# Where the first loads are issued, and how the decay rows are formed, in a two-layer hybrid transformer kernel

## The chip, the cores and the metric

The kernel runs on one core of one Trainium2 chip. The metric is the device time of one execution in microseconds (us); the number given for a kernel is the median of its runs. One further execution was taken with the hardware profiler, and all rows below come from that one.

## The reference, cut to what matters

A sequence of 256 rows of width 2048 passes an even and an odd layer. Each layer normalizes its rows, multiplies by one wide weight matrix, runs three kinds of token mixing on slices of the product and multiplies by an output matrix:

```python
def even_layer(x, mem, ...):
    h = rms_norm(x, norm_g) @ w_in
    gq, gk, gv, gb, ga, gg, dq, dk, dv, dg, mq, mg = split_cols(h, EV_SPLITS)
    y = concat([gdn_branch(gq, gk, gv, gb, ga, gg, conv_w, a_log, dt_bias, gdn_gain),
                diff_attention(dq, dk, dv, dg, rel_table, dq_gain, dk_gain, lam, subln, lambda_init),
                memory_attention(mq, mg, mem, mem_norm, mem_w_kv, mem_qn, mem_kn)])
    return x + y @ w_out
# in gdn_branch, per head and chunk:  g = cumsum(g)
diff = g[..., :, None] - g[..., None, :]
decay = where(lower_incl, exp(where(lower_incl, diff, 0.0)), 0.0)
m = where(strict, einsum('bhncd,bhnsd->bhncs', k_beta, k) * decay, 0.0)
t_inv = triangular_solve(eye + m, eye)
a_intra = where(lower_incl, einsum('bhncd,bhnsd->bhncs', q, k) * decay, 0.0)
```

The odd layer has window attention and latent attention with rotary positions (cosines and sines of `positions`) in place of the first two, and memory attention again. `rel_bias` is the table behind the additive attention bias, `mem` the 256 memory rows. All is float32.

## The kernel before

**Products.** Every float32 product is made of three TensorE passes: each operand is split into a rounded high part and the remainder. `gemm` (L206 on) walks a weight matrix in blocks of 512 KB. A block is loaded by SyncE's queue (`load_w`, L194; four buffers `w`), cast to its high part `wh` on ScalarE (L201) and its low part `wl` formed on VectorE (L202; three buffers each), and then feeds 12 matmuls of 128x512: passes L218 (wh with xH), L219 (wl) and L220 (wh with xL). One 512-column product has eight such blocks. `gemm_T` does the same with the roles swapped (L233 to L235, 128x256).

**Order.** The program builds instructions in the order of the text, and a scheduler with its own timeline model then puts each engine's list into a fixed order; each engine, and each engine's DMA queue, takes its list strictly in that order. `tc.issue_after(x)` holds a scheduled instruction behind x. So an edit moves work on all engines, and an instruction that waits holds all that stands behind it on its engine.

**Start.** The transposed activations `xt` and the first weight blocks come through SyncE's queue; ScalarE and VectorE split `xt` into xH and xL (L154, L155). Behind the last split, ScalarE's queue issues the constants `cst` (128x672), a row of gains broadcast to 128 partitions (`bcp`, source `row`, 128x424), `hot`, `wrow`, `rel_bias` (`rbt`), `posi`, and the natural rows `xN` of x, twice 128x2048, for `natural_rms` (L180 to L187: one buffer `xnat`, sum of squares on ScalarE L186, then `inv_sqrt`: VectorE L144 and a power on GpSimd L145). Its result is `rs0`, the row scale. The first three products are the diff attention's q, k and v halves; `normed_T` (L261 on) squares the accumulators with `rs0` as scale (L269), reduces, takes a power on GpSimd, scales and transposes by TensorE. The hot table times `rel_bias` (one matmul, L456) is written to DRAM (L461) and read back as `bias` (L501, 1536 KB). The rotary tables `sn`, `cs` are two Sin on ScalarE (L488, L491), with a table load ahead of them. `mem_split` (L580 on) loads the transposed memory in eight pieces `mt` (two buffers, ScalarE's queue, L585) and splits them; `natural_rms` runs again over `memN`. L646 is the Exp of `ea`.

**Decay.** In the stage of the gated delta net, `keys_decay` runs for two groups of four heads. Per group, for both halves t of the rows and both directions d, it forms E = exp(g_c - g_r + mask): TensorE transposes a column of `gcum` broadcast to 128 columns (L757, tile `pb`), VectorE subtracts and adds the mask (L759, 128x128 each) and ScalarE takes the Exp (L761, 128x512). `pg` (L752) is k times k, and `MnT` (L763) their product. `MnT` of both groups goes through DRAM to a solver of 31 steps on VectorE (L787 on), whose inverses come back into `Tm` and `Rm` (L816, SyncE's queue; `Rm` is zeroed on GpSimd first, L804) for TensorE at L859 and later.

Of the kernel before, what the change touches and what calls it, by code (L numbers as in the profile page):

```python
# [87 lines left out]
def kernel(ctx: ExitStack, tc: tile.TileContext, a: dict, out: bass.AP):  # L88
# [332 lines left out]
    with tc.tile_pool(name="xn", bufs=8) as xn:
# [42 lines left out]
        lm = xn.tile([P, 2, 64], F32, name="lm", bufs=1)
        lv_ = bcp[:, B_LAM:B_LAM + 256].rearrange("p (a b c) -> p a b c", a=2, b=2)
        V.tensor_tensor(lm, lv_[:, :, 0], lv_[:, :, 1], op=ALU.mult)
        ls = spool.tile([P, 2], F32, tag="ls", name="ls")
        V.tensor_reduce(ls, lm, axis=AX.X, op=ALU.add)
        A.activation(ls, ls, AF.Exp)
        V.tensor_tensor(lamn, ls[:, 1:2], ls[:, 0:1], op=ALU.subtract)  # L470
        V.tensor_scalar(lamn, lamn, LAM0, None, op0=ALU.subtract)

        posf = xn.tile([P, 2], F32, name="posf", bufs=1)
        V.tensor_copy(posf, posi)
        ang, kk, red, sn, cs = [xn.tile([P, 2, 32], F32, name=n, bufs=1) for n in ("ang", "kk", "red", "sn", "cs")]
        V.tensor_tensor(ang, bcm(cst[:, C_IF:C_IF + 32], 2), bc3(posf, 32), op=ALU.mult)
        MAGIC = 1.5 * 2.0 ** 23
        V.tensor_scalar(kk, ang, 1.0 / (2 * math.pi), MAGIC, op0=ALU.mult, op1=ALU.add)
# [8 lines left out]
        V.tensor_scalar(red, red, pi_, -pi_, op0=ALU.min, op1=ALU.max)
        A.activation(sn, red, AF.Sin)  # L488
        V.scalar_tensor_tensor(red, red, -1.0, red, op0=ALU.mult, op1=ALU.max)
        V.tensor_scalar(red, red, -1.0, math.pi / 2, op0=ALU.mult, op1=ALU.add)  # L490
        A.activation(cs, red, AF.Sin)  # L491
        for i, (b0, sc_) in enumerate(((B_MQR, 192 ** -0.5), (B_MKR, 1.0))):
            g1, g2 = bcp[:, b0:b0 + 32], bcp[:, b0 + 32:b0 + 64]
            for j, (first, second) in enumerate(((cs, sn), (sn, cs))):
                V.scalar_tensor_tensor(tabs[:, :, 2 * i + j, 0:32], first, sc_, bcm(g1, 2), op0=ALU.mult, op1=ALU.mult)
                V.scalar_tensor_tensor(tabs[:, :, 2 * i + j, 32:64], second, sc_, bcm(g2, 2), op0=ALU.mult, op1=ALU.mult)
# [705 lines left out]
```

## Time and profile before

| | |
|---|---|
| runs | 1205.7, 1206.37, 1207.79 us (median 1206.37) |
| the profiled execution | 1208.67 us, of which the span of its instructions is 1206.9 us |
| granted TensorE clock, mean | 0.996 |
| busy, share of the span | PE 99%, PEld 88%, DVE 70%, ACT 53%, POOL 9% |
| chain that ended last, by engine | PE 89%, DVE 4%, DMA 3%, ACT 2% |

PE is TensorE's matmuls, PEld its weight loads, DVE VectorE, ACT ScalarE, POOL GpSimd, SP SyncE; a small q behind an engine's name is its queue of DMA issues. A matmul's span is modelled and overlaps the next one's, so a stretch with PE at 100% can still hold more or fewer matmuls than another: the number of instructions in a stretch of equal work tells more than the share.

### The profile page before, as it was taken

How to read it: one execution, taken by the hardware profiler on the slowest of the kernel's cores; microseconds unless marked ns; L12 is line 12 of the kernel's file. 1: busy time of each engine (PE TensorE's matmuls, PEld its weight loads, DVE VectorE, ACT ScalarE, POOL GpSimd, SP SyncE). 2: the span in 40 equal slices, each digit the busy share in tenths (PEclk: the TensorE clock that was granted, in tenths of full speed). 3: DMA queues.
4: the chain of work that ended last, by engine and by line, in shares of the span. 5: the costliest groups of instructions: out<-in, count | busy, mean ns of one | idle time of the engine just before them, and what ended most of it. 6: DMA issues, size and time to landing. Idle time of an engine off the chain costs nothing.

```text
span 1206.9 us, 19842 instructions
## 1 busy us (share of the span) xinstructions
PE 1190.3 (99%) x7608; PEld 1063.2 (88%) x7608; DVE 839.8 (70%) x1450; ACT 640.0 (53%) x1117; POOL 109.8 (9%) x116
## 2 busy tenths in 40 slices
PE   9899999999999999999999999999999999999998
PEld 7678888788999999889988889999889899998887
DVE  5675876666889899857755555667766678876553
ACT  6664666455555454444654446566555555554432
POOL 0110112000101010002000001323310000000000
PEclk9899999999999999999999999999999999999999
DMA  9976675555655666653536656666556565555663
GB/s 333 350 225 230 215 236 162 175 165 167 174 152 137 168 176 192 194 142 82 187 105 209 206 167 185 179 184 194 160 158 203 164 208 158 159 157 166 201 210 121
DMA packets 183183, 221.95 MB, mean 184 GB/s; under 512 B 20536, under 2 KB 119608, under 8 KB 182576
## 3 DMA queue, kind: packets, MB, share of 16 engines
q1 hardware_dynamic: 172640, 201.09, 56.0%
q10 hardware_dynamic: 9552, 16.48, 3.9%
q0 software_dynamic: 896, 3.11, 0.8%
q8 instruction: 59, 0.97, 0.3%
q14 instruction: 36, 0.29, 0.1%
HBM read 214.36 MB, written 6.29 MB: 183 GB/s over the span
## 4 chain that ended last, share of the span: by engine, by line
PE 89%; DVE 4%; DMA 3%; ACT 2%; issue 1%; POOL 1%; SPq 0%; DVEq 0%; ACTq 0%; POOLq 0%
PE acc L219 14%; PE acc L220 13%; PE acc L218 13%; PE acc L254 6%; PE acc L256 6%; PE acc L255 6%; PE acc L366 4%; PE acc L367 4%; PE acc L365 4%; PE acc L235 3%; PE acc L233 3%; PE acc L234 3%; PE ps L165 3%; PE ps L892 1%; DVE wl L202 1%
## 5 line engine op out<-in xcount | busy, mean ns | idle before, releaser
L202 DVE TENSOR_TENSOR wl<-w,wh 128x1024 fp32r<-128x1024 f32 (+3 forms) x392 | 456.8, 1167 | 240.5 <-ACT wh L201 237.9
L201 ACT CAST wh<-w 128x1024 fp32r<-128x1024 f32 (+3 forms) x392 | 392.1, 1001 | 401.4 <-PE acc L220 141.3
L219 PE MATMUL acc<-wl,xH 128*128 128x512 f32 (+3 forms) x704 | 259.5, 370 | 3.0 <-DVE wl L202 3.0
L220 PE MATMUL acc<-wh,xL 128*128 128x512 f32 (+3 forms) x704 | 256.0, 365 | 0.0
L218 PE MATMUL acc<-wh,xH 128*128 128x512 f32 (+3 forms) x704 | 238.5, 366 | 2.7 <-ACT wh L201 2.7
L219 PEld LDWEIGHTS acc<-wl,xH 128*128 128x128 f32 x704 | 133.1, 189 | 24.2 <-DVE wl L202 5.4
L218 PEld LDWEIGHTS acc<-wh,xH 128*128 128x128 f32 x704 | 130.5, 189 | 21.1 <-ACT wh L201 4.2
L220 PEld LDWEIGHTS acc<-wh,xL 128*128 128x128 f32 x704 | 133.1, 189 | 17.1
L255 PE MATMUL acc<-wl,y 128*128 128x512 f32 x320 | 124.9, 391 | 0.0
L256 PE MATMUL acc<-wh,y 128*128 128x512 f32 x320 | 124.4, 390 | 0.0
L254 PE MATMUL acc<-wh,y 128*128 128x512 f32 x320 | 115.3, 392 | 1.3 <-ACT y L154 1.3
L235 PE MATMUL acc<-xH,wl 128*128 128x256 f32 x384 | 109.4, 286 | 1.1 <-DVE wl L202 1.1
L365 PE MATMUL acc<-xH,wh 128*128 128x256 f32 x384 | 110.1, 287 | 0.0
L366 PE MATMUL acc<-xL,wh 128*128 128x256 f32 x384 | 109.9, 286 | 0.0
L367 PE MATMUL acc<-xH,wl 128*128 128x256 f32 x384 | 109.6, 286 | 0.0
L233 PE MATMUL acc<-xH,wh 128*128 128x256 f32 x384 | 109.3, 285 | 0.0
L234 PE MATMUL acc<-xL,wh 128*128 128x256 f32 x384 | 109.1, 284 | 0.0
L145 POOL TENSOR_TENSOR r<-isq,kept 128x4 f32<-128x4 f32 (+2 forms) x27 | 49.7, 1841 | 400.4 <-DVE isq L144 384.1
L235 PEld LDWEIGHTS acc<-xH,wl 128*128 128x128 f32 x384 | 73.4, 191 | 1.7 <-DVE wl L202 1.7
L366 PEld LDWEIGHTS acc<-xL,wh 128*128 128x128 f32 x384 | 74.2, 193 | 0.3
L365 PEld LDWEIGHTS acc<-xH,wh 128*128 128x128 f32 x384 | 74.3, 194 | 0.2
L367 PEld LDWEIGHTS acc<-xH,wl 128*128 128x128 f32 x384 | 74.1, 193 | 0.0
(364 smaller groups left out, 1760.9 us busy)
## 6 DMA issues: line engine op xcount, KB each, us to landing
w<-in_ev_w_in_dram SPq DMA_DIRECT2D x136, 512.0 KB, 4.1
w<-in_od_w_in_dram SPq DMA_DIRECT2D x72, 512.0 KB, 3.9
w<-in_ev_w_out_dram SPq DMA_DIRECT2D x40, 512.0 KB, 3.7
w<-in_od_w_out_dram SPq DMA_DIRECT2D x40, 512.0 KB, 4.1
w<-in_od_w_in_dram SPq DMA_DIRECT2D x32, 384.0 KB, 3.4
w<-in_od_mem_w_kv_dram SPq DMA_DIRECT2D x16, 512.0 KB, 3.6
w<-in_ev_mem_w_kv_dram SPq DMA_DIRECT2D x16, 512.0 KB, 3.7
w<-in_od_w_in_dram SPq DMA_DIRECT2D x16, 288.0 KB, 2.9
```

The source lines that it names most:

```text
L201: A.copy(wh[:, :kn * n], w[:, :kn * n])
L202: V.tensor_tensor(wl[:, :kn * n], w[:, :kn * n], wh[:, :kn * n].bitcast(F32), op=ALU.subtract)
L218: T.matmul(o, lhsT=h, rhs=wh[:, k], start=first, stop=False)
L219: T.matmul(o, lhsT=h, rhs=wl[:, k], start=False, stop=False)
L220: T.matmul(o, lhsT=l, rhs=wh[:, k], start=False, stop=last)
L235: T.matmul(o, lhsT=wl[:, k], rhs=H[:, kk], start=False, stop=kk == NK - 1)
L254: T.matmul(acc[t], lhsT=h, rhs=wh[:, k], start=first, stop=False)
L255: T.matmul(acc[t], lhsT=h, rhs=wl[:, k], start=False, stop=False)
L256: T.matmul(acc[t], lhsT=l, rhs=wh[:, k], start=False, stop=last)
L365: T.matmul(acc[i], lhsT=wh[:, k, cs], rhs=H[:, kk], start=kk == 0, stop=False)
L366: T.matmul(acc[i], lhsT=wh[:, k, cs], rhs=L[:, kk], start=False, stop=False)
L367: T.matmul(acc[i], lhsT=wl[:, k, cs], rhs=H[:, kk], start=False, stop=kk == NK - 1)
```

## The change

- `cst`, `row` and `xN` stay on ScalarE's queue, `xN` first, with two buffers for `xnat` so that both halves are issued back to back. `hot`, `wrow`, `rbt` and `posi` go to GpSimd's queue and are no longer held behind the last split.
- The memory pieces `mt` go to GpSimd's queue with eight buffers, held behind the power that forms `rs0` (`first_pow`). Their splits are held behind the norming of the keys (`normed[2]`, `normed[3]`: the third and fourth split that `normed_T` makes). The bias table's store is held behind `first_pow`, its load and `memN` behind `normed[2]`, the rotary tables and lambda behind `normed[3]`.
- E is formed otherwise: `gcum` is transposed once and stored to DRAM (`gc_d`); eight DMAs with a zero partition step load its rows broadcast to 128 partitions (128x512 each, ScalarE's queue); VectorE adds the mask (128x512), and ScalarE takes the Exp with -gcum as its bias (128x128 each).
- The memset of `Tm` is held behind that of the solver's identity.

```diff
+    def natural_rms(rs, src, pool, bufs, eng):
         ss = spool.tile([P, 2], F32, tag="ssx", name="ssx")
+        nat = []
         for t in range(2):
-            n_ = pool.tile([P, D], F32, tag="xnat", name="xnat", bufs=1)
-            A.dma_start(n_, src[t * P:(t + 1) * P, :])
+            nat.append(pool.tile([P, D], F32, tag="xnat", name="xnat", bufs=bufs))
+            eng.dma_start(nat[t], src[t * P:(t + 1) * P, :])
+        for t, n_ in enumerate(nat):
             A.activation(n_, n_, AF.Square, accum_out=ss[:, t:t + 1])
-        inv_sqrt(rs, ss, 1.0 / D, EPS)
+        return inv_sqrt(rs, ss, 1.0 / D, EPS)
...
-            split(src, gain, dst(0, t), dst(1, t))
+            normed.append(split(src, gain, dst(0, t), dst(1, t)))
...
         with tc.issue_after(last.ins):
+            first_pow = natural_rms(rs0, a["xN"], xn, 2, A)
             A.dma_start(cst, a["cst"])
             A.dma_start(bcp, a["row"].to_broadcast([P, B_END]))
-            A.dma_start(hot, a["hot"][0:32])
-            A.dma_start(wrow, a["hot"][32:40])
-            A.dma_start(rbt, a["rel_bias"])
-            A.dma_start(posi, a["positions"].rearrange("o (t p) -> p (o t)", p=P))
-            natural_rms(rs0, a["xN"], xn)
+        for dst, src in ((hot, a["hot"][0:32]), (wrow, a["hot"][32:40]), (rbt, a["rel_bias"]),
+                         (posi, a["positions"].rearrange("o (t p) -> p (o t)", p=P))):
+            G.dma_start(dst, src)
...
-        for i, row in enumerate((brow, wrow)):
-            G.dma_start(bias_d[i], row)
+        with tc.issue_after(first_pow.ins):
+            for i, row in enumerate((brow, wrow)):
+                G.dma_start(bias_d[i], row)
...
-                mt = dp.tile([P, 2, S], F32, tag="mn", name="mt")
-                with tc.issue_after(last.ins):
-                    A.dma_start(mt, mTsrc[:, 2 * g:2 * g + 2])
+                mt = dp.tile([P, 2, S], F32, tag="mn", name="mt", bufs=8)
+                with tc.issue_after(first_pow.ins):
+                    G.dma_start(mt, mTsrc[:, 2 * g:2 * g + 2])
                 for k in range(2):
                     kk = 2 * g + k
-                    split(mt[:, k], par[:, gr + kk:gr + kk + 1], mH[:, kk, :], mL[:, kk, :])
+                    with tc.issue_after(normed[2 + g // 4 if lay == 0 else 0].ins):
+                        split(mt[:, k], par[:, gr + kk:gr + kk + 1], mH[:, kk, :], mL[:, kk, :])
             if lay == 0:
-                with tc.issue_after(last.ins):
-                    natural_rms(rsm, a["memN"], dp)
+                with tc.issue_after(normed[2].ins):
+                    natural_rms(rsm, a["memN"], dp, 1, A)
...
+            ngcum = sm("ngcum")
+            V.tensor_scalar(ngcum, gcum, -1.0, None, op0=ALU.mult)
+            pt = ps_tile()
+            T.transpose(pt[:32, :P], gcum, ident)
+            gr = dp.tile([32, P], F32, name="gr", bufs=1)
+            V.tensor_copy(gr, pt[:32, :P])
+            G.dma_start(gc_d, gr)
...
+        E = gp.tile([P, 2, 2, 4, P], F32, tag="E", name="E", bufs=2)
+        for t in range(2):
+            for d in range(2):
+                r_ = gc_d[t * 16 + d * 8 + h0:t * 16 + d * 8 + h0 + 4]
+                with tc.issue_after(weighed[-1].ins):
+                    A.dma_start(E[:, d, t].rearrange("p h c -> p (h c)"), bass.AP(r_.tensor, r_.offset, [[0, P], [1, 4 * P]]))
...
             for d in range(2):
-                pb = ps_tile()
+                V.tensor_tensor(E[:, d, t], E[:, d, t], bcm(amask(d), 4), op=ALU.add)
                 for h in range(4):
-                    T.transpose(pb[:, h * P:(h + 1) * P], cols(gcum, t, d)[:, h:h + 1].to_broadcast([P, P]), ident)
-                for h in range(4):
-                    V.scalar_tensor_tensor(E[:, d, t, h], pb[:, h * P:(h + 1) * P], cols(gcum, t, d)[:, h:h + 1],
-                                           amask(d), op0=ALU.subtract, op1=ALU.add)
-                A.activation(E[:, d, t], E[:, d, t], AF.Exp)
+                    A.activation(E[:, d, t, h], E[:, d, t, h], AF.Exp, bias=cols(ngcum, t, d)[:, h:h + 1])
...
-        G.memset(Tm, 0.0)
+        with tc.issue_after(eye.ins):
+            G.memset(Tm, 0.0)
```

The scheduler then puts the lists into a new order. The rows below are the engines' fixed lists: line, operation, what it writes and reads, size. First ScalarE at the start, before, from the Exp of `ea` that waits for its constants (L646) to the cast of the weight block after the rotary Sin:

```order
L646 ACTIVATE kept<-kept 128x16
L585 DMA mt<-in_memT_dram 128x2x256
L201 CAST wh<-w 128x1024
L445 DMA wrow<-in_hot_dram 8x512
L469 ACTIVATE ls<-ls 128x2
L186 ACTIVATE xnat,ssx<-xnat 128x2048
L201 CAST wh<-w 128x1024
L185 DMA xnat<-in_xN_dram 128x2048
L186 ACTIVATE xnat,ssx<-xnat 128x2048
L488 ACT_TABLE_LOAD
L488 ACTIVATE sn<-red 128x64
L201 CAST wh<-w 128x1024
```

And ScalarE at the same place with the change, from the loads of `cst` and `row` (both `xN` stand just ahead of them) to the first splits of q. L188 is the sum of squares of `xN`, L273 the square that reads `rs0`; the cast ahead of the second L188 is that of the keys' first block:

```order
L448 DMA kept<-in_cst_dram 128x672
L449 DMA kept<-in_row_dram 128x424
L203 CAST wh<-w 128x1024
L188 ACTIVATE xnat,ssx<-xnat 128x2048
L203 CAST wh<-w 128x1024
L188 ACTIVATE xnat,ssx<-xnat 128x2048
L273 ACTIVATE sq<-acc,kept 128x512 x2
L203 CAST wh<-w 128x1024 x8
L154 ACTIVATE qT<-acc,kept 128x4x128 x2
```

The Sin and its table load, the memory's sums and the Exp of `ea` have left this place; the two squares that read `rs0` now stand ahead of eight casts, the first of them that of the keys' second block. In the list before, those squares stood five casts further on.

VectorE with the change, between the low parts of the weight blocks: `ang` reads `cst` and `posi`, `lm` reads `row`, and `isq` is the step of `rs0`:

```order
L204 TENSOR_TENSOR wl<-w,wh 128x1024 x3
L658 TENSOR_TENSOR ang<-kept,posf 128x64
L660 TENSOR_SCALAR kk<-ang 128x64
L661 TENSOR_SCALAR kk<-kk 128x64
L647 TENSOR_TENSOR lm<-kept 128x128
L665 SCALAR_TENSOR_TENSOR red<-kk,ang 128x64
L144 TENSOR_SCALAR isq<-ssx 128x2
```

So `rs0` stands behind the landings of `cst` and `row` too, and not of `xN` alone.

ScalarE with the change in the stage of the decay; L759 are the broadcasting loads of E, L780 the Exp, L203 the casts of weight blocks:

```order
L759 DMA E<-gc_d 128x512 x7
L736 ACTIVATE sqs<-ps 128x512
L739 COPY kN<-ps 128x512
L780 ACTIVATE E<-E,kept 128x128 x3
L736 ACTIVATE sqs<-ps 128x512
L739 COPY kN<-ps 128x512
L780 ACTIVATE E<-E,kept 128x128
L721 ACTIVATE kT<-cc 128x256
L203 CAST wh<-w 128x1024
L780 ACTIVATE E<-E,kept 128x128 x4
```

Seven loads are issued at once. On VectorE seven of the eight mask additions stand ahead of the low part of the block cast here, and on ScalarE 28 of the 32 Exp stand between this cast and the next.

## Rows read from the trace of the kernel before

**Rows 1.** The page: busy times; bytes moved, in 40 slices of 30.2 us.
```profile
PE 1190.3 (99%) x7608; PEld 1063.2 (88%) x7608; DVE 839.8 (70%) x1450; ACT 640.0 (53%) x1117; POOL 109.8 (9%) x116
...
GB/s 333 350 225 230 215 236 162 175 165 167 174 152 137 168 176 192 194 142 82 187 105 209 206 167 185 179 184 194 160 158 203 164 208 158 159 157 166 201 210 121
```

**Rows 2.** Waits of PE, whole run: total us, times, longest us.
```profile
PE acc L219 <- DVE wl L202: 3.0, 5, 1.0
PE acc L218 <- ACT wh L201: 2.7, 3, 1.9
PE ps L859 <- DMA Rm<-r_d: 2.3, 1, 2.3
```

**Rows 3.** Windows: us, busy by engine PE, PEld, DVE, ACT, POOL, then PEclk, DMA share, GB/s.
```profile
10.00:20.00 10.00, 10.00 (x45) 8.02 (x44) 9.71 (x16) 8.86 (x16) 0.00 (x0) 1.00 1.07 375
20.00:30.00 10.00, 10.00 (x45) 7.89 (x43) 3.98 (x7) 3.46 (x6) 0.00 (x0) 1.00 1.03 348
30.00:40.00 10.00, 7.18 (x28) 4.44 (x26) 6.88 (x22) 8.62 (x14) 1.28 (x2) 0.96 1.03 392
40.00:50.00 10.00, 9.96 (x31) 8.03 (x32) 7.12 (x15) 9.04 (x12) 0.72 (x1) 0.69 1.03 376
350.00:400.00 50.00, 50.00 (x428) 50.00 (x427) 48.07 (x130) 28.70 (x47) 4.58 (x2) 1.00 0.56 148
520.00:530.00 10.00, 8.15 (x191) 7.84 (x192) 4.83 (x7) 2.65 (x6) 0.00 (x0) 0.83 0.52 147
```

**Rows 4.** Timeline of PE: start, us, engine, line, tiles, count, [idle before <- releaser].
```profile
33.57 0.62 PE L218 MATMUL acc<-wh,xH 128*128 128x512 f32 x2
...
38.35 0.73 PE L218 MATMUL acc<-wh,xH 128*128 128x512 f32 x2 [1.90 <-ACT wh L201]
...
40.04 0.80 PE L219 MATMUL acc<-wl,xH 128*128 128x512 f32 x1 [0.96 <-DVE wl L202]
```

**Rows 5.** Timeline of ACT, 27 to 38 us.
```profile
27.88 0.22 ACT L646 ACTIVATE kept<-kept 128x16 f32<-128x16 f32 x1 [5.37 <-DMA xnat<-in_xN_dram]
...
37.27 1.03 ACT L201 CAST wh<-w 128x1024 fp32r<-128x1024 f32 x1
```

**Rows 6.** Waits of SyncE's queue, 0 to 70 us.
```profile
SPq L194 <- DMA posi<-in_positions_dram: 5.7, 1, 5.7
```

**Rows 7.** DMA issues, 0 to 70 us: count, KB each, median us to landing.
```profile
w<-in_ev_w_in_dram SPq DMA_DIRECT2D x24, 512.0 KB, 6.2
...
xnat<-in_xN_dram ACTq DMA_DIRECT2D x2, 1024.0 KB, 9.1
...
bias<-bias_d ACTq DMA_DIRECT2D x1, 1536.0 KB, 10.2
...
kept<-in_row_dram ACTq DMA_DIRECT2D x1, 212.0 KB, 5.4
```

**Rows 8.** Timeline of POOL, 34 to 46 us.
```profile
39.16 0.54 POOL L461 DMA_DIRECT2D bias_d<-wrow  x1 [3.73 <-DVE wrow L459]
44.69 0.72 POOL L145 TENSOR_TENSOR kept<-isq,kept 128x2 f32<-128x2 f32 x1 [4.99 <-DVE isq L144]
```

**Rows 9.** Groups by line and shape: busy us, mean ns of one, idle before.
```profile
L759 DVE SCALAR_TENSOR_TENSOR E<-ps,kept 128x128 f32<-128x128 f32 x32 | 9.0, 353 | 0.3 <-PE ps L757 0.3
L761 ACT ACTIVATE E<-E 128x512 f32<-128x512 f32 x8 | 4.9, 625 | 0.9 <-DVE E L759 0.9
L828 DVE TENSOR_TENSOR E<-ps,E 128x512 f32<-128x512 f32 x8 | 5.0, 680 | 0.0
```

**Rows 10.** Timeline of PE around the first transposes of `gcum`.
```profile
368.25 0.60 PE L757 MATMUL ps<-kept 128*128 128x128 f32 x4
...
368.80 0.28 PE L235 MATMUL acc<-xH,wl 128*128 128x256 f32 x1
```

**Rows 11.** Timeline of DVE: the second group's `MnT`, ahead of the solver.
```profile
397.06 4.24 DVE L763 SCALAR_TENSOR_TENSOR MnT<-ps,kept,E 128x128 f32<-128x128 f32 x16
```

**Rows 12.** Timeline of PE: the first use of the solver's `Rm`.
```profile
521.85 0.95 PE L859 MATMUL ps<-X,Rm 32*32 32x32 f32 x48 [2.32 <-DMA Rm<-r_d]
```

More of the change, by code (lines that the diff above doesn't have):

```diff
@@ L412 @@
     bias_d = dpool.tile([2, 8, 512], F32, name="bias_d")
+    gc_d = dpool.tile([32, P], F32, name="gc_d")
     NG = 480
@@ L459 @@
         V.tensor_tensor(wrow, wrow, brow, op=ALU.add)
-        for i, row in enumerate((brow, wrow)):
-            G.dma_start(bias_d[i], row)
[L464 to L478, printed above, removed]
@@ L487 @@
[L487 to L496, printed above, removed]
+        with tc.issue_after(first_pow.ins):
+            for i, row in enumerate((brow, wrow)):
+                G.dma_start(bias_d[i], row)
@@ L645, in gdn_rates @@
             ea = keep(16)
-            A.activation(ea, bcp[:, B_AL:B_AL + 16], AF.Exp)
+            with tc.issue_after(normed[1].ins):
+                A.activation(ea, bcp[:, B_AL:B_AL + 16], AF.Exp)
             V.scalar_tensor_tensor(v2(gl), v2(z), -1.0, bcm(ea, 2), op0=ALU.mult, op1=ALU.mult)
@@ new lines @@
+        qkv = diff_qkv(0)
+        lm = dp.tile([P, 2, 64], F32, name="lm", bufs=1)
+        lv_ = bcp[:, B_LAM:B_LAM + 256].rearrange("p (a b c) -> p a b c", a=2, b=2)
+        V.tensor_tensor(lm, lv_[:, :, 0], lv_[:, :, 1], op=ALU.mult)
+        ls = spool.tile([P, 2], F32, tag="ls", name="ls")
+        V.tensor_reduce(ls, lm, axis=AX.X, op=ALU.add)
+        with tc.issue_after(normed[3].ins):
+            A.activation(ls, ls, AF.Exp)
+        V.tensor_tensor(lamn, ls[:, 1:2], ls[:, 0:1], op=ALU.subtract)
@@ new lines @@
+        V.tensor_scalar(lamn, lamn, LAM0, None, op0=ALU.subtract)
+        posf = dp.tile([P, 2], F32, name="posf", bufs=1)
+        V.tensor_copy(posf, posi)
+        ang, kk, red, sn, cs, ab = [dp.tile([P, 2, 32], F32, name=n, bufs=1) for n in ("ang", "kk", "red", "sn", "cs", "ab")]
+        V.tensor_tensor(ang, bcm(cst[:, C_IF:C_IF + 32], 2), bc3(posf, 32), op=ALU.mult)
+        MAGIC = 1.5 * 2.0 ** 23
+        V.tensor_scalar(kk, ang, 1.0 / (2 * math.pi), MAGIC, op0=ALU.mult, op1=ALU.add)
+        V.tensor_scalar(kk, kk, MAGIC, None, op0=ALU.subtract)
@@ new lines @@
+        c1 = 6.28125
+        c2 = float(np.float32(np.round((2 * math.pi - c1) * 2.0 ** 21) / 2.0 ** 21))
+        c3 = 2 * math.pi - c1 - c2
+        V.scalar_tensor_tensor(red, kk, -c1, ang, op0=ALU.mult, op1=ALU.add)
+        V.scalar_tensor_tensor(red, kk, -c2, red, op0=ALU.mult, op1=ALU.add)
+        V.scalar_tensor_tensor(red, kk, -c3, red, op0=ALU.mult, op1=ALU.add)
+        pi_ = float(np.nextafter(np.float32(math.pi), np.float32(0)))
+        V.tensor_scalar(red, red, pi_, -pi_, op0=ALU.min, op1=ALU.max)
@@ new lines @@
+        V.scalar_tensor_tensor(ab, red, -1.0, red, op0=ALU.mult, op1=ALU.max)
+        V.tensor_scalar(ab, ab, -1.0, math.pi / 2, op0=ALU.mult, op1=ALU.add)
+        with tc.issue_after(normed[3].ins):
+            A.activation(sn, red, AF.Sin)
+            A.activation(cs, ab, AF.Sin)
+        for i, (b0, sc_) in enumerate(((B_MQR, 192 ** -0.5), (B_MKR, 1.0))):
+            g1, g2 = bcp[:, b0:b0 + 32], bcp[:, b0 + 32:b0 + 64]
+            for j, (first, second) in enumerate(((cs, sn), (sn, cs))):
+                V.scalar_tensor_tensor(tabs[:, :, 2 * i + j, 0:32], first, sc_, bcm(g1, 2), op0=ALU.mult, op1=ALU.mult)
+                V.scalar_tensor_tensor(tabs[:, :, 2 * i + j, 32:64], second, sc_, bcm(g2, 2), op0=ALU.mult, op1=ALU.mult)
@@ L664 @@
+        with tc.issue_after(normed[2].ins):
+            load_bias(bias, 0)
         mem_split(0)
-        rsb, beta, nbeta, gl, gcum, e1, ne1, e2, be2 = gdn_rates()
+        rsb, beta, nbeta, ngcum, e1, ne1, be2 = gdn_rates()
         diff_attention(0, *qkv)
```

20 lines of the change are left out of this document (5 added, 15 removed).

## The prediction

> **What bounds the kernel now.** I read the page first: TensorE is busy for 1190.3 of 1206.9 us, no other engine for over 70% [rows 1]. So time is won in two ways only: fewer TensorE instructions, or less waiting by TensorE. Its waits by name are few, and three are of a size to matter: for a weight block's low part, for its high part, and once for the solver's `Rm` [rows 2]. The windows tell what that list leaves out, because a matmul at a slow clock counts as busy. At full clock 45 matmuls of 128x512 go into 10 us, 0.222 us each; from 30 to 40 us there are 28, from 40 to 50 us 31 at a granted clock of 0.69 [rows 3]. The clock has the levels 1.2 and 2.4 GHz, and 0.69 is a mean of the two: the low one was granted for part of that stretch, right behind TensorE's waits. The timeline shows these. The block after the one at 33.57 was due 12 x 0.222 later, at 36.2, and came at 38.35: 2.1 us late, for a cast on ScalarE; 1.0 more went at 40.04 for the low part [rows 4]. With the 14 matmuls that are short from 40 to 50 us (3.1 us) the place costs **6.2 us**. Its cause lies upstream. ScalarE takes its list in order, and a small Exp waited 5.4 us for a load at 27.88; the late cast began only at 37.27 [rows 5]. SyncE's queue was held 5.7 us by `posi`'s landing [rows 6]. And the DMA engines were full from 10 to 50 us, at 348 to 392 GB/s with a share above 1 [rows 3].
> The second place is the solver's end. TensorE reached L859 2.3 us before `Rm` had landed [rows 12], and from 520 to 530 us the clock averaged 0.83, 1.7 us in 10 [rows 3]: together **4.0 us**.
>
> **The change part by part.** The sum is made against the profiled execution, 1208.67 us; that is 2.3 above the median of the runs, so I put the same differences on the median, 1206.37.
>
> *A, the transposes.* 32 transposes (L757) go, one comes. Four of them and one pass of 128x256 take from 368.25 to 368.80, 0.55 us [rows 10]; a TensorE instruction in this stretch takes 50/428 = 0.117 us [rows 3]; so one transpose takes (0.55 - 0.117)/4 = 0.108. TensorE was busy throughout [rows 3], nothing hid them: 31 x 0.108 = **-3.3 us**. On VectorE 32 instructions of some 0.28 (9.0 us in all) become eight like L828's, 5.0 in all [rows 9]. On ScalarE eight Exp of 0.63 [rows 9] become 32 of a quarter of the columns, whose price no row shows: between 0.16, a quarter of 0.63, and 0.63. I take 0.27, close to the 0.22 that an Exp of 16 columns took [rows 5]: 8.6 us instead of 5, where ScalarE was busy 28.7 of 50 [rows 3].
>
> *B, the start.* The Sin, its table load and the memory's sums leave ScalarE's list there, and `posi` no longer holds SyncE's queue. But the squares of q, which need `rs0`, now stand ahead of the cast for the keys' second block, and `rs0` needs both `xN`, `cst` and `row`. In the kernel before, `rs0` was formed only at 45.4 [rows 8], but the squares stood five casts further on. So what matters is when the loads land. Needed up to `row` are `xt` 2.1 MB, `xN` 2.1, `cst` 0.34, `row` 0.22, 0.2 of small ones, and nine weight blocks of 0.52 to which the four buffers add up to four: 9.7 to 11.8 MB. The first slice of 30.2 us moved 333 GB/s, 10.1 MB [rows 1], and after it 392 GB/s flow [rows 3]: between 29.2 and 34.6 us, and about 32.2 in the middle. Then come the small steps and the power, 0.72 [rows 8], 1.2 in all; two squares of 0.63, as for the Exp of that size [rows 9]; and a cast of 1.03 [rows 5]. That cast ends at 35.7, where its block is due at 33.6 (the hot product, ahead of it before, is only moved): 2.1 us late, between 0 and 4.5. The low part adds 1.0 as before, and as the clock fell behind just such a wait I count the 3.1 again. That is 6.2 against 6.2: **0**, between -6.2 and +2.4. The other waits for weight blocks, 0.8 and 2.0 us in the run [rows 2], may go, since SyncE's queue is less held, or grow, since 14 splits of the memory now stand between casts of v; at 0.5 us for such a split I bound this by -2 and +3 and take 0.
>
> GpSimd's queue gets 16 loads `mt`, four small ones and `gc_d`. An issue took 0.54 [rows 8]; seven `mt` then stand between `rs0`'s power and the q power, 3.8 us, and the eighth and the second store of the bias table wait for landings. The q power is wanted only after seven more key blocks of 2.7 us, so this costs nothing; if landings took over 10 us more, the q transposes would wait. The bias table, 10.2 us on its way [rows 7], is issued behind the keys' norming and first read by the attention, a whole v product of 8 x 2.7 us and more later: hidden.
>
> *C, the solver.* Before, VectorE was busy 48.07 of 50 us there [rows 3], and the second group's `MnT` ended at 401.3 [rows 11], 120.5 us ahead of L859. It loses 4.0 us of work ahead of `MnT` (part A), and E is formed before the product `pg` instead of after it; TensorE's own gain lies ahead of `pg`, so it moves both ends alike. 4.0 exceeds 2.3: the wait should go, and with it the slow stretch, **-4.0 us**. The bounds are -4.0 and 0.
>
> *D, the new loads.* Seven loads of 256 KB, each a row repeated on 128 partitions, are issued together, and in list order VectorE's mask additions and then 28 Exp (7.6 us at 0.27) stand ahead of casts and low parts that TensorE wants some 12 and 16 us later. The nearest rows for their way: a broadcast of 212 KB took 5.4 us and 1.5 MB from the same kind of scratch 10.2, both with the DMA engines full [rows 7]; here the share is 0.56 at 148 GB/s [rows 3]. By the first nothing waits, by the second, scaled to 1.8 MB, they land after 12.2 us, and the low part is late by some 3. I take **+1.2**, nearer to the first since the engines are half free; bounds 0 and +11 (third rival).
> The Trainium skill, "DMA: Bandwidth & Descriptors", section "Anatomy of one DMA", gives for a DMA issued from GpSimd 2.0 us plus a microsecond for every 436 KB. These loads are issued from ScalarE, so taking it over is an estimate: 1.8 MB would be there after 6.2 us, D would be 0 and the time 1199.1. The rows are slower than that rule (512 KB in 6.2 us against 3.2) [rows 7], at least where the engines are full.
>
> **Sum:** -3.3 + 0 - 4.0 + 1.2 = -6.1 us; 1208.67 becomes 1202.6, the median 1206.37 becomes **1200.3 us**. The forecast's own range is 1197 to 1203.9.
>
> **The rivals.**
> 1. *Both waits vanish.* The loads land by 30 us, the cast is at most a few tenths late and the clock stays: B is -6.2, the time 1194.1. For it speaks the low end of B, against it that the DMA engines have no room between 10 and 50 us [rows 3].
> 2. *The solver's wait stays,* and the change at the start does not do what it says: the transfers bound there in any order, and only the name of the wait changes. C and B are 0, the time 1204.3, about no change. For it: the 120.5 us behind `MnT` are untouched, and 1.7 us of room, 4.0 less 2.3, is little if weight blocks stand elsewhere in VectorE's new order.
> 3. *Slower: the loads of E hold two engines.* If the seventh lands 14 us after the first is issued, TensorE waits first for the low part behind VectorE's additions, then for the cast behind ScalarE's 28 Exp: 14 + 7.6 + 1.0 + 1.2 less the 16 us until that block is wanted is 7.8 us of waiting, and 3.1 of slow clock behind it. D is then 10.9 and the time 1210.0. It decides from D = 9.7 on, a landing after some 13 us. For it speaks the price of the 1.5 MB; against it the half-free DMA engines, and that the Exp start with the first landing and not with the last.
>
> **How the numbers follow.** A measurement of this kernel can tell about 0.2%, 2.4 us, from no change: faster means under 1204.0, slower over 1208.8. Chances: forecast 0.52, first rival 0.16, second 0.20, third 0.12. Faster takes nearly all of the forecast (0.48), the first rival and 0.06 of the second: 0.70. Same is the rest of the second and a little of the forecast, 0.17; slower the third rival and a hundredth of bad cases at the start, 0.13. The range reaches down past the first rival, 1193.5, and up to 1209.0, where most of the third is left out.
>
> **What would show it.** A: TensorE has 31 instructions fewer and L757 is gone. B: the square that reads `rs0` begins at 33 to 35 us, the cast for the next block ends near 35.7, and the windows from 30 to 50 us again fall short by some 28 matmuls; if they hold 80 or more in all, the first rival is right. C: no wait at L859, clock 1.00 from 520 to 530 us. D: the landings of E within 9 us and a wait for a low part or cast near 365 us under 2 us; waits over 6 us there mean the third rival. I am wrong if the first wait at 33 us is over 5 us, or if TensorE waits longer at L859's place than before.

## The result, and the profile after

The change is **slower**: median 1220.2 us (1217.86 to 1221.83, four runs) against 1206.03 for the kernel before on the same chip, ratio 1.0113 [1.0098, 1.0127], about 13.6 us. The profiled execution took 1220.35 us, its span 1218.6, 11.7 longer than that of before.

The page of the kernel after, the engines' busy times:

```profile
PE 1195.1 (98%) x7577; PEld 1067.1 (88%) x7577; DVE 836.9 (69%) x1428; ACT 644.6 (53%) x1141; POOL 118.2 (10%) x137
```

TensorE has the 31 instructions fewer and is still busy 5 us longer than in [rows 1]. Its waits by name, total us, times, longest (L220 and L221 are L218 and L219 of before, L235 and L237 the same passes of `gemm_T`; L884 is L864, which here uses `Rm` first, as L859 did before):

```profile
PE acc L221 <- DVE wl L204: 5.5, 5, 3.4
PE acc L220 <- ACT wh L203: 3.8, 3, 1.6
PE acc L237 <- DVE wl L204: 3.2, 3, 1.8
PE ps L884 <- DMA Rm<-r_d: 2.1, 1, 2.1
PE acc L235 <- ACT wh L203: 1.7, 1, 1.7
```

The waits for weight blocks have grown, not gone, and the solver's is still there [rows 2]. Windows of the kernel after, columns as in [rows 3]:

```profile
30.00:40.00 10.00, 7.74 (x32) 5.38 (x32) 8.68 (x21) 6.69 (x8) 6.89 (x11) 1.00 0.91 297
40.00:50.00 10.00, 10.00 (x45) 8.26 (x44) 3.48 (x3) 3.96 (x4) 3.69 (x2) 1.00 1.00 336
...
70.00:80.00 10.00, 5.52 (x23) 3.99 (x22) 7.10 (x23) 9.97 (x21) 2.94 (x4) 0.91 0.61 215
80.00:90.00 10.00, 10.00 (x35) 7.93 (x35) 5.86 (x9) 4.51 (x6) 2.89 (x4) 0.75 1.05 379
90.00:100.00 10.00, 7.92 (x31) 5.91 (x30) 4.12 (x5) 6.12 (x6) 0.72 (x1) 0.93 0.81 287
...
380.00:390.00 10.00, 6.31 (x46) 5.72 (x45) 9.96 (x32) 10.00 (x27) 0.41 (x1) 0.94 0.37 81
...
520.00:530.00 10.00, 7.21 (x165) 6.18 (x164) 7.00 (x12) 4.60 (x8) 1.50 (x1) 0.76 0.93 261
530.00:540.00 10.00, 10.00 (x88) 9.68 (x88) 2.15 (x3) 2.21 (x3) 0.00 (x0) 0.73 0.03 10
```

And three windows of the kernel before, which [rows 3] leaves out:

```profile
70.00:80.00 10.00, 10.00 (x50) 8.34 (x49) 8.20 (x12) 6.09 (x10) 0.00 (x0) 1.00 0.87 279
80.00:90.00 10.00, 10.00 (x46) 8.29 (x45) 4.78 (x4) 5.12 (x6) 0.00 (x0) 1.00 0.63 177
90.00:100.00 10.00, 10.00 (x46) 8.29 (x45) 4.02 (x5) 4.22 (x4) 0.00 (x0) 1.00 0.67 208
```

Read down the PE counts. From 30 to 50 us 77 matmuls fit, where there were 59 [rows 3], and in this execution the clock does not fall: the start is better. But there are 23, 35 and 31 from 70 to 100 us, where the kernel before has 50, 46 and 46; against the 45 of 128x512 that fit at full clock, 46 matmuls are missing. ScalarE is busy 9.97 of 10 us in the first of these windows, and again from 380 to 390, where TensorE has 6.31.

To count both waits and slow clock, I took for every matmul the time to the start of the next, less the median of that for its line and shape in the same trace, and summed the excess by place, each under the start of the later matmul. What is left is the work:

| us lost by TensorE | before | after | difference |
|---|---|---|---|
| 25 to 75 us | 8.7 | 3.4 | -5.3 |
| 75 to 125 us | -0.3 | 11.7 | +12.0 |
| 375 to 450 us | 1.9 | 7.3 | +5.4 |
| 500 to 550 us (solver's end) | 4.7 | 8.2 | +3.5 |
| 550 to 650 us | 5.7 | 2.1 | -3.6 |
| work, the sum of the medians | 1176.4 | 1175.3 | -1.1 |
| all other places | | | +0.8 |

The differences sum to +11.7; "all other places" includes the time ahead of the first matmul and behind the last. The experiments use this table.

**From 70 to 100 us.** The timeline of ScalarE after (start, us, engine, line, tiles, count, [idle before <- releaser]), from the start to the decay:

```profile
33.89 1.27 ACT L273 ACTIVATE sq<-acc,kept 128x512 f32<-128x512 f32 x2 [1.29 <-POOL kept L145]
...
68.09 0.59 ACT L151 CAST kT<-acc 128x512 fp32r<-128x512 f32 x1 [1.66 <-PE acc L284]
68.58 2.90 ACT L154 ACTIVATE mH<-mt,kept 128x256 fp32r<-128x256 f32 x7
71.39 0.56 ACT L151 CAST kT<-acc 128x512 fp32r<-128x512 f32 x1
72.07 1.28 ACT L673 ACT_TABLE_LOAD   x1
...
74.47 1.03 ACT L203 CAST wh<-w 128x1024 fp32r<-128x1024 f32 x1
75.41 2.50 ACT L154 ACTIVATE mH<-mt,kept 128x256 fp32r<-128x256 f32 x6
...
94.09 1.92 ACT L188 ACTIVATE xnat<-xnat 128x2048 f32<-128x2048 f32 x1 [2.50 <-DMA xnat<-in_memN_dram]
...
378.74 6.56 ACT L780 ACTIVATE E<-E,kept 128x128 f32<-128x128 f32 x22
385.59 2.00 ACT L203 CAST wh<-w 128x1024 fp32r<-128x1024 f32 x2
```

And VectorE after, same columns:

```profile
71.98 0.69 DVE L152 TENSOR_TENSOR kT<-acc,kT 128x512 fp32r<-128x512 f32 x1 [2.58 <-ACT kT L151]
...
73.66 0.23 DVE L679 SCALAR_TENSOR_TENSOR kept<-sn,kept 128x64 f32<-128x64 f32 x1 [0.92 <-ACT sn L673]
74.81 3.64 DVE L155 SCALAR_TENSOR_TENSOR mL<-mt,kept,mH 128x256 fp32r<-128x256 f32 x9
78.37 1.22 DVE L204 TENSOR_TENSOR wl<-w,wh 128x1024 fp32r<-128x1024 f32 x1
...
377.21 0.69 DVE L778 TENSOR_TENSOR E<-E,kept 128x512 f32<-128x512 f32 x1 [0.24 <-DMA E<-gc_d]
...
382.37 4.22 DVE L782 SCALAR_TENSOR_TENSOR MnT<-ps,kept,E 128x128 f32<-128x128 f32 x16
...
396.74 4.22 DVE L782 SCALAR_TENSOR_TENSOR MnT<-ps,kept,E 128x128 f32<-128x128 f32 x16
```

And TensorE after, same columns:

```profile
36.14 0.73 PE L220 MATMUL acc<-wh,xH 128*128 128x512 f32 x2 [1.13 <-ACT wh L203]
37.41 0.50 PE L221 MATMUL acc<-wl,xH 128*128 128x512 f32 x1 [0.53 <-DVE wl L204]
...
75.56 0.73 PE L220 MATMUL acc<-wh,xH 128*128 128x512 f32 x2 [1.13 <-ACT wh L203]
79.64 0.79 PE L221 MATMUL acc<-wl,xH 128*128 128x512 f32 x1 [3.35 <-DVE wl L204]
...
97.13 0.73 PE L220 MATMUL acc<-wh,xH 128*128 128x512 f32 x2 [1.55 <-ACT wh L203]
...
386.69 0.38 PE L235 MATMUL acc<-xH,wh 128*128 128x256 f32 x1 [1.66 <-ACT wh L203]
...
389.02 0.58 PE L237 MATMUL acc<-xH,wl 128*128 128x256 f32 x1 [1.83 <-DVE wl L204]
...
524.44 0.18 PE L884 MATMUL ps<-Rm,X 32*32 32x32 f32 x1 [2.11 <-DMA Rm<-r_d]
```

Read the three together. At 68.58 the norming of the keys releases the memory's splits, and seven high parts, 2.90 us, run on ScalarE between the two casts of `kT`. VectorE idles 2.58 for the second `kT` and 0.92 for the Sin behind a table load, so its nine low parts (`mL`, 3.64) begin only at 74.81, and the weight block's low part stands behind them, at 78.37. TensorE waits 1.13 and 3.35, and its clock averages 0.75 in the window behind. Then `memN`'s second sum waits 2.50 for its landing with a cast behind it: 1.55 more at 97.13. Of the 11.7 us lost from 75 to 125 us, 6.6 are waits; the rest goes mostly in the windows with a clock of 0.91, 0.75 and 0.93.

### The profile page after: what moved, and what is told of

It reads as the page before. It is cut to its first block, busy times and chain, and to the rows that moved or that the text cites. A ratio compares the mean times of both kernels' runs of the same rounds, so it can differ in the third digit from the quotient of the medians.

```text
span 1218.6 us, 19818 instructions
## 1 busy us (share of the span) xinstructions
PE 1195.1 (98%) x7577; PEld 1067.1 (88%) x7577; DVE 836.9 (69%) x1428; ACT 644.6 (53%) x1141; POOL 118.2 (10%) x137
## 3 DMA queue, kind: packets, MB, share of 16 engines
HBM read 216.46 MB, written 6.31 MB: 183 GB/s over the span
## 4 chain that ended last, share of the span: by engine, by line
PE 56%; DVE 0%; ACT 0%; DVEq 0%; issue 0%
PE acc L220 6%; PE acc L222 6%; PE acc L221 6%; PE acc L256 6%; PE acc L258 6%; PE acc L257 6%; PE acc L369 4%; PE acc L370 4%; PE acc L371 4%; PE ps L165 2%; PE ps L912 1%; PE ps L340 1%; PE ps L1054 1%; PE ps L942 1%; PE ps L892 0%; PE ps L172 0%
## 5 line engine op out<-in xcount | busy, mean ns | idle before, releaser
L203 ACT CAST wh<-w 128x1024 fp32r<-128x1024 f32 (+3 forms) x392 | 391.8, 1001 | 412.1 <-PE acc L222 147.2
L221 PE MATMUL acc<-wl,xH 128*128 128x512 f32 (+3 forms) x704 | 259.8, 370 | 5.5 <-DVE wl L204 5.5
L220 PE MATMUL acc<-wh,xH 128*128 128x512 f32 (+3 forms) x704 | 240.8, 368 | 4.0 <-ACT wh L203 3.8
L221 PEld LDWEIGHTS acc<-wl,xH 128*128 128x128 f32 x704 | 133.3, 189 | 25.3 <-DVE wl L204 7.6
L220 PEld LDWEIGHTS acc<-wh,xH 128*128 128x128 f32 x704 | 131.1, 189 | 24.0 <-ACT wh L203 5.7
L237 PE MATMUL acc<-xH,wl 128*128 128x256 f32 x384 | 109.6, 287 | 3.2 <-DVE wl L204 3.2
L235 PE MATMUL acc<-xH,wh 128*128 128x256 f32 x384 | 109.9, 286 | 1.7 <-ACT wh L203 1.7
L237 PEld LDWEIGHTS acc<-xH,wl 128*128 128x128 f32 x384 | 74.0, 193 | 3.8 <-DVE wl L204 3.8
L235 PEld LDWEIGHTS acc<-xH,wh 128*128 128x128 f32 x384 | 74.3, 193 | 1.9 <-ACT wh L203 1.8
L369 PEld LDWEIGHTS acc<-xH,wh 128*128 128x128 f32 x384 | 74.6, 195 | 0.2
```

The lines of the kernel that those rows point to most:

```text
L203: A.copy(wh[:, :kn * n], w[:, :kn * n])
L220: T.matmul(o, lhsT=h, rhs=wh[:, k], start=first, stop=False)
L221: T.matmul(o, lhsT=h, rhs=wl[:, k], start=False, stop=False)
L235: T.matmul(o, lhsT=wh[:, k], rhs=H[:, kk], start=kk == 0, stop=False)
L237: T.matmul(o, lhsT=wl[:, k], rhs=H[:, kk], start=False, stop=kk == NK - 1)
L369: T.matmul(acc[i], lhsT=wh[:, k, cs], rhs=H[:, kk], start=kk == 0, stop=False)
```

## The experiments

Theory S: the loss from 75 to 125 us is the batch of memory splits that the pins on the keys' norming release between casts. Theory B: the loss from 375 us on is the batch of mask additions and Exp of the decay. A difference between two kernels is taken between their ratios, times 1206.

**e1, the change with the memory's splits not held.**

```diff
-                    with tc.issue_after(normed[2 + g // 4 if lay == 0 else 0].ins):
-                        split(mt[:, k], ...)
+                    split(mt[:, k], ...)
```

> The change, without the pins that hold the memory's splits behind the keys' norming. Theory S (the splits come in a batch between casts and low parts of v's blocks, TensorE waits and then runs at the low clock): the matmuls that 75 to 125 us lack come back, some 12 us, so about 1208 us; TensorE waits under 1.5 us in all from 60 to 105 us. Rival D (memN's and the bias table's loads fill the DMA engines there, the weights come late): the waits from 70 to 100 us stay, 1217 us or more.

Measured: 1209.08 against 1204.25, ratio 1.0028 [1.0015, 1.0042]; 10.2 us under the change. From 75 to 125 us 1.6 is lost instead of 11.7. Waits of TensorE from 60 to 105 us:

```profile
PE acc L221 <- DVE wl L204: 2.0, 3, 0.8
PE acc L220 <- ACT wh L203: 1.3, 2, 0.8
```

The loss goes with the pins, as theory S says. 3.3 us of waits are left there, in pieces of 0.8 at most, which is more than the theory allowed.

**e2, the change with the decay of before**: transposes, subtraction and wide Exp back, no `gc_d`.

```diff
-                V.tensor_tensor(E[:, d, t], E[:, d, t], bcm(amask(d), 4), op=ALU.add)
+                pb = ps_tile()
                 for h in range(4):
-                    A.activation(E[:, d, t, h], ..., AF.Exp, bias=cols(ngcum, t, d)[:, h:h + 1])
+                    T.transpose(pb[:, h * P:(h + 1) * P], ..., ident)
+                for h in range(4):
+                    V.scalar_tensor_tensor(E[:, d, t, h], pb[...], cols(gcum, t, d)[:, h:h + 1], amask(d), ...)
+                A.activation(E[:, d, t], E[:, d, t], AF.Exp)
```

> The change at the start as it is, but the decay rows formed as before (32 transposes, mask on VectorE, eight Exp of 512 columns). Theory B (the burst of 28 Exp holds the casts behind it on ScalarE, TensorE lacks 5.4 us from 375 to 450 us): that loss goes, 3.3 us of transposes come back, so about 1218 us. Rival (the stretch lost its time to the late start, not to the Exp): only the transposes come back, 1223 us.

Measured: 1214.22, ratio 1.0072 [1.0047, 1.0097]: 8.7 us over before, 4.9 under the change. The loss from 375 to 450 us falls from 7.3 to 1.3, and that at the solver's end from 8.2 to 1.4. So the decay part costs more than theory B gave it, which expected some 2 us here. The list at the start is that of the change, yet here the clock fell from 40 to 50 us, where it was 1.00 after; TensorE's waits ahead of that stretch were 3.1 us here and 2.2 after:

```profile
40.00:50.00 10.00, 10.00 (x39) 8.11 (x38) 3.95 (x4) 2.42 (x3) 5.47 (x6) 0.84 0.95 325
```

**e3, the kernel before with the decay part alone** (e2's edit the other way round, and the transpose, store and loads of `gc_d`).

> The kernel before, with only the decay part of the change. Theory B: 5.4 us lost to the burst less 3.3 us of transposes, and the solver's wait stays near 2 us: about 1208 us. Rival (without the late start the burst finds room, and the solver's wait goes): 1203 us or less, as forecast for this part.

Measured: 1207.26, ratio 1.0029 [1.0013, 1.0044], 3.5 us slower. The work fell by 2.0, the solver's wait went to 0.7, but 6.0 is lost from 375 us on instead of 1.9. TensorE of e3 there (L235 and L233 are the passes with wl and wh):

```profile
378.79 0.39 PE L233 MATMUL acc<-xH,wh 128*128 128x256 f32 x1 [1.36 <-ACT wh L201]
...
381.43 0.58 PE L235 MATMUL acc<-xH,wl 128*128 128x256 f32 x1 [2.13 <-DVE wl L202]
```

The same pair of waits as after the change, without its start: the loss belongs to the decay part.

**e4, the start alone**: e1's and e2's edits together.

> The start of the change with free splits, decay rows as before. Theories S and B: what is left of the change is its gain from 25 to 75 us, some 5 us, so about 1201 us. Rival D: the waits from 70 to 100 us stay and the time is over 1210 us.

Measured: 1208.7, ratio 1.0026 [1.0011, 1.004], where 1201 was expected: a miss. From 75 to 125 us the loss is gone (2.1), as theory S has it; but 7.7 is lost from 25 to 75 us, with a clock of 0.86 from 40 to 50. The start's gain, 5.3 us in the profile of the change, was not there.

**e5, the splits spread**: e2 with each pair of splits held behind its own cast of v's eight blocks.

```diff
+        casts.append(A.copy(wh[:, :kn * n], w[:, :kn * n]))
...
-                    with tc.issue_after(normed[2 + g // 4 if lay == 0 else 0].ins):
+                    with tc.issue_after((casts[16 + g] if lay == 0 else normed[0]).ins):
```

> As e2_decay_old, but each pair of the memory's splits held only behind one cast of v's eight weight blocks (one pair a block) and not behind the keys' norming. Theory S (it is the batch that costs, not the splits): the 11 us that e2 lacks from 75 to 125 us go and the start keeps its gain from 25 to 75 us; against before, which took 1204.3 beside the last runs, about 1202 us. Rival (16 splits more in the lists cost the same wherever they stand there, as the 3 us that e4 lost): 1207 us.

Measured: 1205.82 against 1205.05, ratio 1.0007 [0.9994, 1.002]: equal to before, and 8 us under e2, between the 1202 of the theory and the 1207 of the rival. Of the 11.3 us that e2 lost from 75 to 125 us, 2.7 are left with one pair at a time, and the start kept its gain (3.3 lost); but 4.8 went at the solver's end, where e2 lost 1.4. A window of e5:

```profile
70.00:80.00 10.00, 10.00 (x50) 8.35 (x49) 6.88 (x19) 5.54 (x10) 1.47 (x3) 1.00 0.95 342
```

In place of 23 matmuls in that window there are 50 (some of a smaller shape), at full clock.

**e6, e3 with eight wide Exp**: VectorE adds -gcum and the mask in one instruction per head.

```diff
-                V.tensor_tensor(E[:, d, t], E[:, d, t], bcm(amask(d), 4), op=ALU.add)
                 for h in range(4):
-                    A.activation(E[:, d, t, h], ..., AF.Exp, bias=cols(ngcum, t, d)[:, h:h + 1])
+                    V.scalar_tensor_tensor(E[:, d, t, h], E[:, d, t, h], cols(ngcum, t, d)[:, h:h + 1],
+                                           amask(d), op0=ALU.add, op1=ALU.add)
+                A.activation(E[:, d, t], E[:, d, t], AF.Exp)
```

> As e3_decay_alone (the kernel before with only the decay part), but -gcum is added with the mask on VectorE, 32 instructions of 128x128 as before the change, and ScalarE takes eight Exp of 128x512. The loads of E stay. Theory B (the 28 Exp hold the casts): the 6 us that e3 lacks from 375 to 400 us go, at most 1 us of them stays, so about 1202 us. Rival (the loads' landings hold VectorE's list, and with it the low parts): the 6 us stay, 1208 us.

Measured: 1206.41, ratio 1.0009 [0.9991, 1.0026], 2.4 us under e3, between the 1202 of theory B and the 1208 of the rival. From 375 to 450 us 3.2 is lost instead of 6.0, but 3.8 at the solver's end instead of 0.7. With ScalarE's Exp shortened most of the loss in the decay went (before had 1.9 there), but most of what was won came back as waiting at the solver's end.

**e7, e5's start with e6's decay.**

> The change with the splits spread as in e5 and the decay as in e6. If both theories hold, the gain of the start and the transposes' 2.8 us add up: about 1199 us beside 1204 of before, the fastest of all. If the losses come back in another place, over 1203 us.

Measured: 1207.77, ratio 1.0024 [1.0009, 1.0039], where 1199 was expected: a miss. The two gains don't add. Its profile has a new wait of 2.5 us at 413 us, which ends with one of the solver's steps on VectorE (`Rm<-Rm,tmp`), 2.5 at the solver's end, and a clock of 0.83 from 40 to 50 us.

**e8, e5 with the squares of q later**: the keys' product is built ahead of the norming of q, whose squares are held behind the eleventh cast. The new order of the two holds for both halves of the diff attention, the pin for the first alone.

```diff
+            both = []
-            for nm_, col, gain, dst in (("q", EV["dq"], gmix[:, 0:1], qT), ("k", EV["dk"], None, kT)):
+            for col in (EV["dq"], EV["dk"]):
                 gemm(w0, col + 512 * half, 512, xH, xL, ...)
-                normed_T(pss, rs0, ...)
+                both.append(pss)
+            for pss, gain, dst in zip(both, (gmix[:, 0:1], None), (qT, kT)):
+                normed_T(pss, rs0, ..., casts[10] if half == 0 and dst is qT else None)
```

> As e5_splits_spread, with q's two squares that read rs0 moved behind the casts of the keys' second and third blocks. If TensorE's waits at 31 to 37 us come from the cast that stands behind those squares, at least 2 of their 2.9 us go: about 1203 us beside 1205 of before, and no slow clock at 40 us. Rival (VectorE's list waits for the same landings ahead of the low part, so the wait only changes its name): the waits stay at 2 us or more, 1206 us.

Measured: 1201.05 against 1206.62, ratio 0.9959 [0.9947, 0.9972]: faster than both kernels. But not for the reason given: from 33 to 40 us there are 2.4 us of waits, where e5 has 2.2. As the rival says, the wait changed its name: 1.14 for the cast behind the squares is gone, and 1.18 for a low part stands in its place (below, in e11's rows, too).

**e9, the kernel before once more.**

> The kernel before, unchanged, for a second profile. Theory (the slow clock at 40 us in the profile of before was that execution's own: its 1208.7 us lies at the upper end of before's runs): the clock is 1.00 from 40 to 50 us and the span some 3 us shorter. Rival (the fall belongs to the kernel): 0.69 again.

Measured, in one execution: 1205.06, span 1203.3. Windows of this second profile:

```profile
40.00:50.00 10.00, 9.04 (x32) 7.04 (x33) 8.70 (x17) 9.14 (x13) 1.26 (x2) 0.83 1.01 357
...
520.00:530.00 10.00, 10.00 (x239) 9.60 (x233) 6.85 (x12) 4.08 (x7) 0.00 (x0) 1.00 0.47 153
```

The clock falls again from 40 to 50 us, but to 0.83 and not 0.69. The solver's wait, 2.3 us in [rows 2], was 0.5 here, and the clock behind it stayed at 1.00: at the solver's end 1.6 us is lost instead of 4.7. One profile of one program is no fixed price for either.

**e10, e3 with the Exp held behind the group's last copy of `kN`,** so that the casts pass them.

```diff
+                    with tc.issue_after(copies[-1].ins):
+                        A.activation(E[:, d, t, h], ..., AF.Exp, bias=cols(ngcum, t, d)[:, h:h + 1])
```

> As e3_decay_alone, loads and mask additions unchanged, but the Exp of a group held behind that group's last copy of k on ScalarE, which puts two casts of weight blocks ahead of the second group's 16. Theory B (the Exp hold the casts): of the 6 us that e3 lacks from 375 to 400 us at most 2 stay. Rival (landings and VectorE's additions hold the low parts): 5 us or more stay.

Measured: 1210.0, ratio 1.0031 [1.0016, 1.0047]: no better than e3, with 5.0 lost from 375 to 450 us, as the rival has it. VectorE of e10, and then TensorE:

```profile
375.67 4.22 DVE L776 SCALAR_TENSOR_TENSOR MnT<-ps,kept,E 128x128 f32<-128x128 f32 x16
379.80 1.21 DVE L202 TENSOR_TENSOR wl<-w,wh 128x1024 fp32r<-128x1024 f32 x1
```

```profile
381.07 0.39 PE L235 MATMUL acc<-xH,wl 128*128 128x256 f32 x1 [2.04 <-DVE wl L202]
```

The casts came early, at 373.27 and 374.62, but the low part stood behind 16 `MnT` in a row, and not behind landings or additions. Theory B named only half of it: VectorE's batch holds TensorE as ScalarE's does, and moving one uncovers the other.

**e11 and e12, e8 and e5 again, side by side on one chip.**

> e8_squares_later once more, beside e12, for a second profile on one chip. Theory (the later squares let the clock stay up and the solver's end come in time, beyond the waits at 31 to 40 us, which kept 2.9 us in e8's profile): 4 us under e12 again, no slow clock before 60 us. Rival (the difference of e8 and e5 was one of chips and executions): within 1.5 us of e12.

> e5_splits_spread once more, beside e11, for a second profile on one chip. Theory: as before within 2 us of the kernel before, 4 us over e11, with a slow clock before 60 us in its profile or a wait of 2 us at the solver's end. Rival: within 1.5 us of e11.

Measured: e11 1202.0, ratio 0.9977 [0.9964, 0.999]; e12 1205.29, ratio 1.0003 [0.9994, 1.0012]. The gain of e8 over e5 is there again, 3.1 us. TensorE of e11:

```profile
31.88 0.73 PE L221 MATMUL acc<-wh,xH 128*128 128x512 f32 x2 [0.59 <-ACT wh L204]
33.13 0.50 PE L222 MATMUL acc<-wl,xH 128*128 128x512 f32 x1 [0.53 <-DVE wl L205]
...
37.79 0.50 PE L222 MATMUL acc<-wl,xH 128*128 128x512 f32 x1 [1.18 <-DVE wl L205]
...
514.44 1.41 PE L875 MATMUL ps<-X,Rm 32*32 32x32 f32 x62 [1.00 <-DMA Rm<-r_d]
```

The early waits stand in e11 too, and the clock was 1.00 from 40 to 50 us in both, so the gain is not there. Between these two profiles it is spread over 75 to 125 us (0.8 lost instead of 1.7), the solver's end (2.4 instead of 4.2) and the attention's scores (7.62 us in all instead of 8.15). The same three differ between e8 and e5 (1.4 instead of 2.7, 1.7 instead of 4.8, and again 7.62 instead of 8.15). How the edit brings them about stays open.

The table of lost time, with the experiments:

| us lost by TensorE | before | e9 | after | e1 | e2 | e3 | e4 | e5 | e6 | e7 | e8 | e10 | e11 | e12 |
|---|---|---|---|---|---|---|---|---|---|---|---|---|---|---|
| 25 to 75 | 8.7 | 7.5 | 3.4 | 6.8 | 5.9 | 6.1 | 7.7 | 3.3 | 7.8 | 5.4 | 3.3 | 7.6 | 3.2 | 3.6 |
| 75 to 125 | -0.3 | -0.3 | 11.7 | 1.6 | 11.3 | 0.0 | 2.1 | 2.7 | 0.0 | 1.6 | 1.4 | 0.0 | 0.8 | 1.7 |
| 375 to 450 | 1.9 | 1.4 | 7.3 | 6.9 | 1.3 | 6.0 | 1.2 | 1.0 | 3.2 | 4.2 | 1.2 | 5.0 | 1.0 | 1.2 |
| 500 to 550 | 4.7 | 1.6 | 8.2 | 2.6 | 1.4 | 0.7 | 4.9 | 4.8 | 3.8 | 6.6 | 1.7 | 3.6 | 2.4 | 4.2 |

Read it by rows. The first is 3.2 to 7.7 in the nine profiles with the start of the change, 4.7 in the mean, and 6.1 to 8.7 in the five with that of before, 7.5 in the mean. The second is large only in after and e2, which hold the splits as the change does. The third is at least 3.2 wherever E comes through DRAM, and at most 1.9 elsewhere. The fourth follows neither part.

## Why the prediction was wrong

**The step that failed** is the one sentence of part B on the memory: "14 splits of the memory now stand between casts of v; at 0.5 us for such a split I bound this by -2 and +3 and take 0". It measured +12.0 us in the profiles, and e1 gives 10.2 back by undoing those pins alone. The price of one split was about right (seven high parts in 2.90 us, 0.41 each). What was missing:
- The batch runs on two engines. I priced it on ScalarE only; the low parts stand in VectorE's list as well, ahead of a weight block's low part, and that wait is the larger one, 3.35 against 1.13.
- The batch holds others of its own stage. It sits between two casts of `kT`, so VectorE idles 2.58 us and begins its own share late. The sum of durations understates it.
- The clock fell behind the waits, as [rows 3] already showed at the start. I counted that for the waits I priced, not for a wait I had bounded at +3.

**A was right.** 31 instructions went; taking the 32 transposes by the time each kept the next from starting, they were 2.8 us of work against -3.3, and e3's work fell by 2.0 net. In the kernel after the work fell by only 1.1, because the small products of 32x32 and 64x64 behind the solver took 1.8 more by their medians (1.1 more in e3, at full clock); why is open.

**B's first half had the order right and its price too high.** The square that reads `rs0` began at 33.89 (33 to 35 forecast), and TensorE waited 1.13 and 0.53 behind it, where 2.1 and 1.0 were forecast. The slow clock counted behind them did not come in this execution, so 25 to 75 us gained 5.3 where 0 was forecast; the 77 matmuls from 30 to 50 us lie near the 80 of the first rival. The size of that gain is in part luck: e2, e4 and e7 have such a fall of the clock, after, e1, e5, e8, e11 and e12 have not. By the means of the table it is some 3 us.

**C failed.** "4.0 exceeds 2.3: the wait should go"; it was 2.11, with a clock of 0.76 and 0.73 behind it, and the place lost 3.5 more. From the last `pg` (393.8, before 386.7) to the end of `MnT` the way did get shorter, from 14.6 to 7.2 us. But TensorE's own work from that `pg` to the use of `Rm` shrank too, by 4.5, because the new list has less between the two, 938 matmuls instead of 976. And the way from `MnT` through the solver and back grew from 120.5 to 123.5. I compared two numbers on one side of a race and took the other as fixed: 7.4 less 4.5 and 2.9 leaves nothing. The 2.3 I started from was itself one execution's number (e9: 0.5).

**D was undersized**, +1.2 against +5.4 in the profiles. The decay part as a whole cost 3.5 us alone (e3) and 4.9 within the change (e2). One Exp took 6.56/22 = 0.30 us, near the 0.27 taken. The third rival had the mechanism, two held engines, at twice its price and with the wrong cause. It made everything hang on the seventh landing. The eight loads had a median of 6.2 us:

```profile
E<-gc_d ACTq DMA_DIRECT2D x8, 256.0 KB, 6.2
```

The additions lost little to them:

```profile
L778 DVE TENSOR_TENSOR E<-E,kept 128x512 f32<-128x512 f32 x8 | 5.4, 688 | 2.1 <-DMA E<-gc_d 2.0
```

2.0 us of idle time in all, 1.3 of it ahead of the first. The 6.56 us of Exp ahead of a cast did the rest, and the 16 `MnT` ahead of the low part ended as late (386.59) as that cast; e6 and e10 show the two batches from either side. My reason for a small D, "since the engines are half free", was a mean over 50 us. While the loads ran the DMA engines were full; a window of the kernel after, columns as above:

```profile
370.00:375.00 5.00, 5.00 (x46) 5.00 (x45) 3.16 (x7) 3.15 (x9) 0.00 (x0) 1.00 0.97 265
```

The share is 0.97 at 265 GB/s.

The Trainium skill, "DMA: Bandwidth & Descriptors", section "Anatomy of one DMA", would by the estimate in the prediction have had seven of these loads there 6.2 us after the first issue, with D at 0. The measurement decides against it here: the first was issued at 367.77, the seventh not before 371, and the fifth addition still waited for a load until 377.21, 9.4 us later. Loads by that rule would still have left the Exp ahead of the casts; no run here shows what D would then be.

**The sum.** The first half of the start -5.3, splits +12.0, decay +5.4, solver +3.5 and work -1.1 make +14.5; 550 to 650 us gave back 3.6, and the rest is +0.8. In that stretch the kernel before has three waits, 1.3 for the high part of `y`, 1.0 for `MnT` and 0.7 for a low part, and the kernel after has none; what removed them was not tried.

**What stays open.** Why e8's version is some 3 to 6 us faster than e5's; whether breaking up the 16 `MnT` as well would make the decay part pay (not tried); and why the clock falls in some executions of one list and not in others.

## What to carry to other kernels

A pin that releases many instructions at once is priced on every engine that takes part, and by what stands behind the batch in each of those lists: the same sixteen splits cost 8 us more in a batch than in pairs between casts (e2, e5). A wait at the meeting of two long chains moves with both of them, so a change of it is priced with the new lengths of both sides; a second profile of the same program tells how much of it is there at all. Where two parts of a change share engines, run them together before adding their gains: e5's and e6's did not add (e7).
